# Own SBUF buffers for weight sums made by transfers, with masks and temporaries moved between SBUF regions, in a two-layer hybrid attention and SwiGLU kernel

## The chip, the cores and the metric

The kernel runs on one core of one Trainium2 chip. The metric is the device time of one execution in microseconds (us). A core has a matrix engine (TensorE, "PE" in the profile), a vector engine (VectorE, "DVE"), an activation engine (ScalarE, "ACT"), a general engine (GpSimd, "POOL") and a queue engine (SyncE, "SP"). Each works through its own instructions in the order that the program gave them. Data moves between the device memory and the on-chip memory SBUF by DMA. Plain transfers are issued on SP here; transfers that add to what lies in SBUF are issued on POOL. PE writes into PSUM, which the code divides into eight banks.

## What is computed

Two layers (`DEPTH = 2`) work on 256 tokens of width 2048, in float32. Each has a token mixer of two attention groups, an output projection, a layer norm, a SwiGLU feed-forward part (FFN) of width 5632, and a second layer norm.

```python
def reference(x, positions, w_in, ...):
    for i in range(DEPTH):
        mix = _hybrid_mixer(x, positions, w_in[i], ...)
        x = _layer_norm(ALPHA * x + mix, ln1_g[i], ln1_b[i])
        ffn = _swiglu(x, w_gate[i], w_up[i], w_down[i])
        x = _layer_norm(ALPHA * x + ffn, ln2_g[i], ln2_b[i])
    return x

def _swiglu(x, w_gate, w_up, w_down):
    h = jax.nn.silu(jnp.einsum('bsd,df->bsf', x, w_gate)) * jnp.einsum('bsd,df->bsf', x, w_up)
    return jnp.einsum('bsf,fd->bsd', h, w_down)
```

The mixer makes one input projection. Group A is attention over the 64 best keys that a small indexer picks for each query; group B is latent attention, in which the latent vectors `cq` and `ckv` are normalised by their root mean square and projected up to queries, keys and values.

## The kernel before

**Three products for one.** A float32 matmul is made of matmuls on parts: `split` (L361) and `parts` (L309) have ACT round a tile to a high part (`wh`, `xh`) and DVE subtract it to get the low part (`wl`, `xl`). Each product is then high x high, high x low and low x high, three matmuls on PE into one PSUM bank (L339 to L341 in projections, L921 to L924 in the FFN's first half).

**Weights.** A weight unit is 128 x 1024 float32 (512 KB, two blocks of 128 rows by 512 columns). `load_raw` (L303) takes a buffer under the tag `raw` and loads it on SP (L306); `parts` turns it into `wh` and `wl` (L317 on ACT, L318 on DVE), buffers of the tags `wh` and `wl`. `raw` has four buffers in the pool `sb`, which lives for the whole kernel. In the phase `more` (FFN and the end of the output projection) two more `raw` lie in that phase's own pool, and `some` (L295) decides in turn whether a unit gets one of the four or one of the two.

**Phases.** `turn(name)` (L100) closes the pool of the last phase and opens the next one in the same part of SBUF: `att` for attention, `more` for the rest of the layer. A buffer of the new phase can be written only when what lay there is done with. `pt` (L109) takes tiles in `att`. Temporaries of 2 KB in a partition come from `t2` (L116): five buffers in `sb`, and in the phase `att` six more, given out in turn. In the FFN the temporaries are the down projection's `d`, the gains `g` and `b`, and the operands `av` and `sv` of the sums on the token side.

**The FFN.** The 5632 hidden columns go in 11 chunks of 512. For chunk 0 gate and up are plain projections. For the other chunks `gate_up` works in quads. A quad takes blocks of two k units (`u` and `u + HALF`) of gate and up for both token tiles. A plain quad (`N`) makes eight products of two k blocks. A summed quad (`S`, `wino_quad`, L947) makes seven products by a Strassen-Winograd scheme, from sums of weights and sums of tokens. It needs four weight tiles: `r12`, which is the up weights of `u` plus those of `u + HALF`, and three plain ones, `r11`, `r21`, `r22`. `r12` is loaded plainly on SP, and then a second transfer on POOL adds the other unit to it (L951). DVE forms the further sums in place: L975 writes `r12 + r11` to `r11`, L979 and L987 the next two. Each of the seven tiles goes through `parts` and then into six matmuls. Chunk 1 has the order NNNS, chunk 2 NSNS, the other eight SSNS.

The last quad of a chunk also combines the products in PSUM into gate and up (`on`, L961, writing `g` and `e`), which frees the banks. `hidden` (L883) then applies SiLU, multiplies and transposes. From chunk 3 on, `down_half` puts a part of the down projection ahead of each chunk: two of four output columns, each of four units, for a pair of earlier chunks. Its results go from PSUM by ACT to `d` (L1025), and POOL issues a transfer that adds `d` to `x` (L1026).

**Attention.** `cmask` and `selmask` (128 x 256) are the causal masks; they lie in the pool `const` for the whole kernel and are made once by `constants()` (L175), called after the first projection of layer 0. Latent vectors are normalised (`rms`, L570), transposed on PE and split by `rms_out` (L584) into `ckvT` and `cqT`; `dup_out` (L555) writes `kpT` from the same PSUM bank as `ckvT`. The indexer's many small DVE operations run in the same stretch.

**Order.** A scheduler lays the instructions of each engine in a fixed order before the run. It goes by the order of the program as a priority, raised by `tc.high_priority(offset=n)`, by when inputs and buffers are free in its own model, and inserts all waits. `tasks` (L264) are generators by which pieces of attention and of norms are laid between the units of projections.

Of the kernel before, what the change touches and what calls it, by code (L numbers as in the profile page):

```python
# [23 lines left out]
F32 = mybir.dt.float32  # L24
# [7 lines left out]
P = 128  # L32
D = 2048
S = 256
# [20 lines left out]
NFC = FFN // C  # L55
RAW = 4
UNITS, MORE = 5, 3
RAWMORE = 2
HALF = NKT // KU // 2
SOONER = 60  # L60
SOON = 200
FIRSTD = 3
T2, T2MORE = 5, 6


QI0, TA, QI1, TB, KA0, QA0, VA0, KA1, QA1, VA1 = range(10)
# [14 lines left out]
def hybrid_trunk(ctx: ExitStack, tc: tile.TileContext, x, xt_in, pos, w_in, g_cq, g_ckv, w_uq,  # L81
# [8 lines left out]
    def nm(s):  # L90
        uid[0] += 1
        return f"{s}{uid[0]}"
# [73 lines left out]
            nc.sync.dma_start(xt[t], x[t * P:(t + 1) * P, :])  # L166

    ident = const.tile([P, P], F32, name="ident")
    cmask = const.tile([P, S], F32, name="cmask")
    selmask = const.tile([P, S], F32, name="selmask")  # L170
    mhalf = const.tile([P, 1], F32, name="mhalf")

    make_identity(nc, ident)

    def constants():  # L175
        nc.gpsimd.memset(cmask, 0.0)
        nc.gpsimd.affine_select(out=cmask[:, P:], in_=cmask[:, P:], compare_op=ALU.is_ge, fill=MASKED,
                                base=0, pattern=[[-1, P]], channel_multiplier=1)
        nc.vector.tensor_scalar(selmask, cmask, 1.0 / 3.0, -BIG, ALU.mult, ALU.add)
        nc.gpsimd.memset(mhalf, -0.5)  # L180

    def causal(m, t):
        return m if t else m[:, P:]
# [119 lines left out]
    def load_raw(src, n):  # L303
        pool, bufs = some("raw", RAW, RAWMORE)
        raw = pool.tile([P, KU * C], F32, name=nm("raw"), tag="raw", bufs=bufs)
        nc.sync.dma_start(raw[:, :n], src)  # L306
        return raw

    def parts(raw, n, own=None):  # L309
# [51 lines left out]
    def split(hi, lo, src):  # L361
        nc.scalar.activation(hi, src, AF.Copy)
        nc.vector.tensor_tensor(lo, src, f(hi), op=ALU.subtract)
# [148 lines left out]
    def layer(l, xh, xl, norms, last):  # L512
# [70 lines left out]

        def rms_out(n, dst, t, tp):  # L584
            tv = tp[:, :n].rearrange("p (k t) -> p k t", t=P)
            split(dst[:, 0, :, t * P:(t + 1) * P], dst[:, 1, :, t * P:(t + 1) * P], tv)

        def tb_post(o):
            gq = t2([P, QL], "gq")
# [21 lines left out]
        def indexer():  # L611
            yield from behind(p_ta, p_qi0, p_qi1)
            score = [pt([P, P * (t + 1)], F32, f"score{t}") for t in range(NT)]
            for t in range(NT):
                n = P * (t + 1)
                per = C // n
                for h0 in range(0, I_HEADS, 2 * per):
                    rp = att()
                    for j in range(per):
                        for r in range(2):  # L620
                            h = h0 + 2 * j + r
                            pr = slice(64 * r, 64 * r + 64)
                            mm(rp[:, r, j * n:(j + 1) * n], qiT[h // 8][pr, h // 2 % 4, t * P:(t + 1) * P],
                               kiT[pr, :n], start=True, stop=True)
                    rl = []
                    for r in range(2):
                        s = t2([P, per, n], "rel")
                        nc.scalar.activation(s.rearrange("p j n -> p (j n)"), rp[:, r, :], AF.Relu)
                        rl.append(s)
                    for j in range(per):  # L630
                        for r in range(2):
                            h = h0 + 2 * j + r
                            nc.vector.scalar_tensor_tensor(
                                score[t], rl[r][:, j, :], wi[t][:, h:h + 1],
                                causal(cmask, t) if h == 0 else score[t], op0=ALU.mult, op1=ALU.add)
                    yield 2
            for t in range(NT):
                for _ in range(TOPK // 8):
                    m8 = small([P, 8], "m8")
                    nc.vector.max(m8, score[t])  # L640
                    nc.vector.match_replace(score[t], m8, score[t], TAKEN)
                    yield 1
                nc.vector.tensor_scalar(bias[t], score[t], (MASKED + TAKEN) / 2, BIG, ALU.is_le, ALU.mult)
                nc.vector.tensor_tensor(bias[t], bias[t], causal(selmask, t), op=ALU.add)

        def cqk(t, k):
            return cqT[:, 0, k, t * P:(t + 1) * P], cqT[:, 1, k, t * P:(t + 1) * P]
# [34 lines left out]
        def mla_attend(hp, m, wait, *before):  # L682

            yield wait
            yield from behind(*before)
            qn, kn, vb = m
            if "B" not in oT:
                oT["B"] = [t8([P, M_HEADS, S], F32R, "oB") for _ in range(2)]

            def logits(h0, dst):  # L690


                ts = [slice(t * P, (t + 1) * P) for t in range(NT)]
                for j in range(2):
                    for t in range(NT):
                        h = (h0 + j) % 4
                        mm(dst[j][t], qn[:, h, ts[t]], kn[:, h, :P * (t + 1)], start=t == 0, stop=False)
                for t in range(NT):
                    for j in range(2):
                        pr = slice(64 * j, 64 * j + 64)  # L700
                        mm(dst[j][t], qpT[pr, h0 // 2, ts[t]], kpT[pr, :P * (t + 1)], start=False, stop=t == NT - 1)

            h0 = 2 * hp
            yield from attend(logits, M_SCALE, [causal(cmask, t) for t in range(NT)],
                              lambda h: (vb[:, 0, (h % 4) * P:(h % 4 + 1) * P], vb[:, 1, (h % 4) * P:(h % 4 + 1) * P]),
                              oT["B"][0][:, h0:h0 + 2, :], oT["B"][1][:, h0:h0 + 2, :], h0)

# [36 lines left out]
        qi_whole = t8([P, I_HEADS // 2, S], F32, "qiT")  # L744
        qiT = [qi_whole[:, 0:4, :], qi_whole[:, 4:8, :]]
        if l == 0:
            o = in_chunk(QI0, load_xT)
            constants()
            rope_tables()
        else:  # L750
            o = in_chunk(QI0, None, lambda: finish(*norms))
        p_qi0 = spawn(heads_T(o, 8, I_DIM, I_ROT, cosI, sinI, qiT[0]))
        turn("att")
        kiT, kpT = pt([P, S], F32, "kiT"), pt([P, S], F32, "kpT")
        wi = [pt([P, I_HEADS], F32, "wi", bufs=2) for _ in range(NT)]
        cq = [pt([P, QL], F32, "cq", bufs=2) for _ in range(NT)]
# [148 lines left out]
        def gate_up(fc, order, between):  # L905
# [40 lines left out]

            def wino_quad(u, final):  # L947
                ADD, SUB = ALU.add, ALU.subtract

                r12 = load_raw(w_gu[1][l, fc, u], KU * C)  # L950
                nc.gpsimd.dma_start(r12, w_gu[1][l, fc, u + HALF], accum_op=ADD)  # L951
                r11, r21, r22 = (load_raw(w_gu[i][l, fc, v], KU * C) for i, v in ((0, u), (0, u + HALF), (1, u + HALF)))

                def p(i, lhs, raw, ks):
                    w = parts(raw, KU * C)
                    name = INTO.get(i, i)
                    passes(name, lhs, ks, w, final)

                def on(d, x, y, op):
                    with tc.high_priority(offset=SOONER):  # L960
                        nc.vector.tensor_tensor(d, x, y, op=op)  # L961

                if final:
                    e = phase["pool"].tile([P, NT, C], F32, name=nm("e"), tag="e", bufs=1)
                    g = phase["pool"].tile([P, NT, C], F32, name=nm("g"), tag="silu", bufs=1)
                lo_, hi_ = unit(u), unit(u + HALF)
                p("p1", token(0), r11, lo_)
                if final:
                    with tc.high_priority(offset=SOONER):
                        nc.scalar.activation(e[:, 0, :], o["p1"], AF.Copy)  # L970
                p("p2", token(0), r21, hi_)
                if final:
                    on(g[:, 0, :], e[:, 0, :], o["c11"], ADD)
                tick()
                nc.vector.tensor_tensor(r11, r12, r11, op=ADD)  # L975
                p("p6", slhs("s2"), r11, lo_)
                if final:
                    on(e[:, 0, :], o["p6"], e[:, 0, :], SUB)
                nc.vector.tensor_tensor(r21, r11, r21, op=ADD)  # L979
                p("p7", slhs("s3"), r12, lo_)  # L980
                if final:
                    on(e[:, 1, :], e[:, 0, :], o["p7"], ADD)
                tick()
                p("p4", token(1), r21, hi_)
                if final:
                    on(g[:, 1, :], o["c21"], e[:, 1, :], SUB)
                nc.vector.tensor_tensor(r11, r11, r22, op=SUB)  # L987
                p("p5", slhs("s1"), r11, lo_)
                if final:
                    on(e, e, o["p5"].unsqueeze(1).to_broadcast([P, NT, C]), ADD)  # L990
                tick()
                p("p3", slhs("s4"), r22, lo_)
                if final:
                    on(e, e, o["up"], ADD)
                tick()
                if final:
                    return g, e
# [141 lines left out]
```

## Time and profile before

| | us |
|---|---|
| median of 3 runs (2223.49 to 2227.57) | 2225.21 |
| the profiled execution | 2224.56 |
| its span | 2222.8 |
| PE busy in it | 2169.5 |
| DVE busy | 1739.8 |
| ACT busy | 1233.2 |
| POOL busy | 154.4 |

The slices of the page show the DMA engines' mean busy share and the bytes per second in 40 equal stretches of 55.6 us:

```profile
DMA  8544456667787787778845445665687787787885
GB/s 297 168 161 152 152 188 216 201 189 229 230 239 222 227 259 220 234 224 231 252 141 162 162 155 186 199 210 199 189 243 238 236 244 239 225 259 219 252 289 140
```

How to read the views: a row of instructions has the line in the code, the engine, the operation and what it writes and reads by the program's tile names; `xN` is the count. In brackets or behind an arrow stands how long the engine was idle just before, and what released it. A row of a waits view says who waited for whom, the total in us, how often, and the longest. A row of the view by stages has the stretch, its length, each engine's busy time with its number of instructions, PE's granted clock, the busy share of the DMA engines and the GB/s.

### The profile page before, as it was taken

What the parts mean: (1) busy time and instruction counts of PE and PEld (TensorE: products, weight loads), DVE (VectorE), ACT (ScalarE), POOL (GpSimd) and SP (SyncE); (2) the same over time, 40 slices, a digit from 0 to 9 for tenths busy, and PEclk for the clock granted to TensorE, in tenths of its full rate; (3) what the DMA queues carried; (4) which work ended last, traced back from release to release, by engine and by line L of the source; (5) the groups of instructions that cost most, each with busy time, mean ns of one, the idle gap of its engine ahead of it and who ended that gap; (6) DMA issues with size and microseconds to landing.
All of it is one profiled execution on the core that took longest, in us unless ns stands there. A gap on an engine that the chain in (4) does not pass through costs nothing. (4 is left out here: it accounts for less than half of the span.)

```text
span 2222.8 us, 28085 instructions
## 1 busy us (share of the span) xinstructions
PE 2169.5 (98%) x10044; PEld 1787.7 (80%) x10044; DVE 1739.8 (78%) x2226; ACT 1233.2 (55%) x1619; POOL 154.4 (7%) x252
## 2 busy tenths in 40 slices
PE   8999999999999999999999999999999999999997
PEld 7888888888777877877888888888888778877776
DVE  6685557898887889888666857678898888889885
ACT  5555554655555566556455555446565566556653
POOL 0100000100000110100101000000001000110101
PEclk9999999999999999999999999999999999999999
DMA  8544456667787787778845445665687787787885
GB/s 297 168 161 152 152 188 216 201 189 229 230 239 222 227 259 220 234 224 231 252 141 162 162 155 186 199 210 199 189 243 238 236 244 239 225 259 219 252 289 140
DMA packets 136365, 471.15 MB, mean 212 GB/s; under 512 B 15408, under 2 KB 15712, under 8 KB 135584
## 3 DMA queue, kind: packets, MB, share of 16 engines
q1 hardware_dynamic: 113760, 409.13, 54.4%
q0 software_dynamic: 22320, 60.09, 14.1%
q8 instruction: 79, 1.29, 0.2%
q14 instruction: 62, 0.51, 0.1%
q10 hardware_dynamic: 144, 0.13, 0.0%
HBM read 445.69 MB, written 2.10 MB: 201 GB/s over the span
## 5 line engine op out<-in xcount | busy, mean ns | idle before, releaser
L317 ACT ACTIVATE wh<-raw 128x1024 fp32r<-128x1024 f32 (+1 forms) x918 | 944.0, 1053 | 809.5 <-PE acc L341 213.3
L318 DVE TENSOR_TENSOR wl<-raw,wh 128x1024 fp32r<-128x1024 f32 (+1 forms) x918 | 1093.5, 1217 | 292.7 <-ACT wh L317 289.6
L339 PE MATMUL acc<-wh,xh 128*128 128x512 f32 (+1 forms) x768 | 304.1, 396 | 6.2 <-ACT wh L317 6.2
L341 PE MATMUL acc<-wh,xl 128*128 128x512 f32 (+1 forms) x768 | 298.9, 389 | 0.5 <-DVE xl L405 0.5
L340 PE MATMUL acc<-wl,xh 128*128 128x512 f32 (+1 forms) x768 | 298.3, 388 | 0.0
L339 PE MATMUL acc<-wh,hT 128*128 128x512 f32 x640 | 252.9, 395 | 18.9 <-DVE e L961 16.6
L341 PE MATMUL acc<-wh,hT 128*128 128x512 f32 x640 | 249.9, 391 | 0.0
L340 PE MATMUL acc<-wl,hT 128*128 128x512 f32 x640 | 249.8, 390 | 0.0
L339 PEld LDWEIGHTS acc<-wh,xh 128*128 128x128 f32 x768 | 145.4, 189 | 37.0 <-ACT wh L317 6.2
L341 PEld LDWEIGHTS acc<-wh,xl 128*128 128x128 f32 x768 | 145.2, 189 | 29.2 <-DVE xl L405 1.3
L340 PEld LDWEIGHTS acc<-wl,xh 128*128 128x128 f32 x768 | 145.4, 189 | 27.2 <-DVE wl L318 1.2
L923 PE MATMUL gu_c<-wl,xh 128*128 128x512 f32 x424 | 165.4, 390 | 0.3 <-DVE wl L318 0.3
L921 PE MATMUL gu_c<-wh,xh 128*128 128x512 f32 x424 | 165.0, 389 | 0.0
L924 PE MATMUL gu_c<-wh,xl 128*128 128x512 f32 x424 | 165.0, 389 | 0.0
L339 PEld LDWEIGHTS acc<-wh,hT 128*128 128x128 f32 x640 | 120.4, 188 | 55.3 <-ACT wh L317 18.2
L341 PEld LDWEIGHTS acc<-wh,hT 128*128 128x128 f32 x640 | 120.6, 188 | 25.4
L975 DVE TENSOR_TENSOR raw<-raw,raw 128x1024 f32<-128x1024 f32 x54 | 66.1, 1223 | 94.9 <-DMA raw<-in_w_up_dram 94.9
L340 PEld LDWEIGHTS acc<-wl,hT 128*128 128x128 f32 x640 | 120.6, 188 | 24.1
L951 POOL DMA_DIRECT2D raw<-in_w_up_dram x54 | 46.1, 853 | 988.8 <-DMA raw<-in_w_up_dram 435.9
L923 PE MATMUL gu_p<-wl,many 128*128 128x512 f32 x228 | 90.8, 398 | 9.2 <-DVE wl L318 9.1
L923 PEld LDWEIGHTS gu_c<-wl,xh 128*128 128x128 f32 x424 | 79.6, 188 | 18.4 <-DVE wl L318 1.9
L921 PEld LDWEIGHTS gu_c<-wh,xh 128*128 128x128 f32 x424 | 79.6, 188 | 16.6
(285 smaller groups left out, 3424.3 us busy)
## 6 DMA issues: line engine op xcount, KB each, us to landing
raw<-in_w_gate_dram SPq DMA_DIRECT2D x176, 512.0 KB, 5.5
raw<-in_w_up_dram SPq DMA_DIRECT2D x176, 512.0 KB, 5.1
raw<-in_w_down_dram SPq DMA_DIRECT2D x176, 512.0 KB, 5.0
raw<-in_w_in_dram SPq DMA_DIRECT2D x144, 512.0 KB, 3.5
raw<-in_w_o_dram SPq DMA_DIRECT2D x64, 512.0 KB, 4.2
raw<-in_w_up_dram POOLq DMA_DIRECT2D x54, 512.0 KB, 8.1
x<-d POOLq DMA_DIRECT2D x80, 256.0 KB, 7.8
raw<-in_w_in_dram SPq DMA_DIRECT2D x16, 400.0 KB, 3.1
```

What stands on the lines that cost most here:

```text
L317: nc.scalar.activation(wh[:, :n], raw[:, :n], AF.Copy)
L318: nc.vector.tensor_tensor(wl[:, :n], raw[:, :n], f(wh[:, :n]), op=ALU.subtract)
L339: mm(o[t][:, :n], h, a, start=first, stop=False)
L340: mm(o[t][:, :n], h, b, start=False, stop=False)
L341: mm(o[t][:, :n], l, a, start=False, stop=final)
L921: mm(o[name], h, a, start=name not in begun, stop=False)
L923: mm(o[name], h, b, start=False, stop=False)
L924: mm(o[name], l, a, start=False, stop=end)
L951: nc.gpsimd.dma_start(r12, w_gu[1][l, fc, u + HALF], accum_op=ADD)
L975: nc.vector.tensor_tensor(r11, r12, r11, op=ADD)
```

## The change

Four things change.

- In `more` the plain `raw` buffers are four and one instead of four and two. The tile `r12` no longer comes from them: `load_sum` takes it from two buffers of their own, tag `sum`, in that phase's pool, with the same two transfers.
- The temporaries of `t2` are four in `sb` and seven in `att`, instead of five and six.
- The masks move from `const` to the pool of `att`, and `make_masks` builds them in each layer. For this, `turn("att")` stands ahead of the first projection in layer 0, and in layer 1 behind it but ahead of the heads' rotation.
- The splits in `rms_out` get a higher priority (`SOON` is 200).

```diff
 UNITS, MORE = 5, 3
-RAWMORE = 2
+RAWMORE, RAWSUM = 1, 2
...
-T2, T2MORE = 5, 6
+T2, T2MORE = 4, 7
...
-    cmask = const.tile([P, S], F32, name="cmask")
-    selmask = const.tile([P, S], F32, name="selmask")
+    masks = {}
...
-    def constants():
+    def make_masks():
+        cmask, selmask = (pt([P, S], F32, s) for s in ("cmask", "selmask"))
+        masks.update(c=cmask, sel=selmask)
         nc.gpsimd.memset(cmask, 0.0)
...
         nc.vector.tensor_scalar(selmask, cmask, 1.0 / 3.0, -BIG, ALU.mult, ALU.add)
-        nc.gpsimd.memset(mhalf, -0.5)
...
+    def load_sum(a, b):
+
+        raw = phase["pool"].tile([P, KU * C], F32, name=nm("sum"), tag="sum", bufs=RAWSUM)
+        nc.sync.dma_start(raw, a)
+        nc.gpsimd.dma_start(raw, b, accum_op=ALU.add)
+        return raw
...
         def rms_out(n, dst, t, tp):
             tv = tp[:, :n].rearrange("p (k t) -> p k t", t=P)
-            split(dst[:, 0, :, t * P:(t + 1) * P], dst[:, 1, :, t * P:(t + 1) * P], tv)
+            with tc.high_priority(offset=SOON):
+                split(dst[:, 0, :, t * P:(t + 1) * P], dst[:, 1, :, t * P:(t + 1) * P], tv)
...
         if l == 0:
+            turn("att")
             o = in_chunk(QI0, load_xT)
-            constants()
+            nc.gpsimd.memset(mhalf, -0.5)
+            make_masks()
             rope_tables()
         else:
             o = in_chunk(QI0, None, lambda: finish(*norms))
+            turn("att")
+            make_masks()
         p_qi0 = spawn(heads_T(o, 8, I_DIM, I_ROT, cosI, sinI, qiT[0]))
-        turn("att")
...
             def wino_quad(u, final):
                 ADD, SUB = ALU.add, ALU.subtract
-
-                r12 = load_raw(w_gu[1][l, fc, u], KU * C)
-                nc.gpsimd.dma_start(r12, w_gu[1][l, fc, u + HALF], accum_op=ADD)
+                r12 = load_sum(w_gu[1][l, fc, u], w_gu[1][l, fc, u + HALF])
```

The three uses of the masks (the indexer's first head, the selection, the latent attention) read `masks["c"]` and `masks["sel"]` instead.

More of the change, by code (lines that the diff above doesn't have):

```diff
@@ L634, in indexer @@
                                 score[t], rl[r][:, j, :], wi[t][:, h:h + 1],
-                                causal(cmask, t) if h == 0 else score[t], op0=ALU.mult, op1=ALU.add)
+                                causal(masks["c"], t) if h == 0 else score[t], op0=ALU.mult, op1=ALU.add)
                     yield 2
@@ L643, in indexer @@
                 nc.vector.tensor_scalar(bias[t], score[t], (MASKED + TAKEN) / 2, BIG, ALU.is_le, ALU.mult)
-                nc.vector.tensor_tensor(bias[t], bias[t], causal(selmask, t), op=ALU.add)
+                nc.vector.tensor_tensor(bias[t], bias[t], causal(masks["sel"], t), op=ALU.add)
         def cqk(t, k):
@@ L703, in mla_attend @@
             h0 = 2 * hp
-            yield from attend(logits, M_SCALE, [causal(cmask, t) for t in range(NT)],
+            yield from attend(logits, M_SCALE, [causal(masks["c"], t) for t in range(NT)],
                               lambda h: (vb[:, 0, (h % 4) * P:(h % 4 + 1) * P], vb[:, 1, (h % 4) * P:(h % 4 + 1) * P]),
```

## The prediction, made before the changed kernel was run

> **What bounds the kernel now.** I read the page first, its busy times and the slices.
>
> ```profile
> span 2222.8 us, 28085 instructions
> PE 2169.5 (98%) x10044; PEld 1787.7 (80%) x10044; DVE 1739.8 (78%) x2226; ACT 1233.2 (55%) x1619; POOL 154.4 (7%) x252
> raw<-in_w_up_dram SPq DMA_DIRECT2D x176, 512.0 KB, 5.1
> raw<-in_w_up_dram POOLq DMA_DIRECT2D x54, 512.0 KB, 8.1
> x<-d POOLq DMA_DIRECT2D x80, 256.0 KB, 7.8
> ```
>
> PE is busy 98% of the span, which looks as if nothing were left. But the ends of matmuls are modelled, so I count starts instead. The timeline of PE around one of the weight sums:
>
> ```profile
> 699.90 0.39 PE L921 MATMUL att<-wh,xh 128*128 128x512 f32 x1
> ...
> 707.84 0.39 PE L924 MATMUL gu_c<-wh,xl 128*128 128x512 f32 x1
> 708.36 0.50 PE L921 MATMUL gu_p<-wh,many 128*128 128x512 f32 x1
> 709.61 0.50 PE L923 MATMUL gu_p<-wl,many 128*128 128x512 f32 x1 [0.76 <-DVE wl L318]
> ```
>
> A matmul of 512 columns lasts 0.39 us in the record, but the next one starts sooner: the first two rows are 35 starts apart without a gap, 7.94 us, so **0.227 us** for each. The gap printed at 709.61 is 0.76 us; by starts PE lost 1.25 - 0.23 = 1.02 us there. So lost PE time is found by counting. The view by stages over most of the two FFNs (520:1080 is layer 0, 1640:2160 layer 1), then two single chunks of layer 0:
>
> ```profile
> 520.00:1080.00 560.00, 539.40 (x2367) 435.46 (x2367) 471.67 (x434) 321.92 (x362) 51.56 (x60) 1.00 0.80 234
> 1640.00:2160.00 520.00, 509.80 (x2251) 416.72 (x2251) 450.20 (x412) 307.91 (x341) 50.66 (x60) 1.00 0.81 243
> 586.60:652.30 65.70, 63.71 (x278) 51.15 (x278) 55.57 (x52) 37.57 (x42) 6.00 (x7) 1.00 0.81 231
> 652.30:719.00 66.70, 63.86 (x279) 51.30 (x279) 55.96 (x52) 37.20 (x42) 6.03 (x7) 1.00 0.79 227
> ```
>
> One chunk is three summed quads (7 products of 6 matmuls), one plain quad (48), two down columns (96) and 8 transposes: 270 matmuls and 8 transposes, the 278 of the third row. At 0.227 us, and 0.11 us for a transpose (the rows at 118.30 to 119.04 below: 7 in 0.74 us), that is 61.3 + 0.9 = 62.2 us, against 65.7 and 66.7 measured. The same count over the long stretches, with 8 transposes in each 278: 528.8 us of work in 560 and 503.4 in 520. **PE loses 31.2 us in the first and 16.6 us in the second, 47.8 together.** Who causes it is in the views of the waits: PE's (first two rows) and DVE's, and DVE's for the same two stretches (the last two pairs, layer 0 then layer 1):
>
> ```profile
> PE acc L339 <- DVE e L961: 16.6, 13, 1.9
> PE gu_p L923 <- DVE wl L318: 9.1, 15, 1.2
> ...
> DVE raw L975 <- DMA raw<-in_w_up_dram: 94.9, 32, 5.7
> ...
> DVE raw L975 <- DMA raw<-in_w_up_dram: 45.0, 14, 5.7
> DVE wl L318 <- ACT wh L317: 36.5, 25, 2.8
> ...
> DVE raw L975 <- DMA raw<-in_w_up_dram: 44.7, 16, 4.9
> DVE wl L318 <- ACT wh L317: 22.4, 22, 3.0
> ```
>
> In these stretches PE waits for DVE nearly always, and DVE's largest own wait is for the sum that L951's accumulating DMA makes. One case, on POOL's, DVE's and PE's timelines:
>
> ```profile
> 694.71 0.85 POOL L951 DMA_DIRECT2D raw<-in_w_up_dram  x1 [18.09 <-DVE wl L318]
> ...
> 705.90 1.22 DVE L975 TENSOR_TENSOR raw<-raw,raw 128x1024 f32<-128x1024 f32 x1 [5.70 <-DMA raw<-in_w_up_dram]
> ...
> 718.11 0.68 DVE L961 TENSOR_TENSOR e<-gu_p,e 128x512 f32<-128x512 f32 x1
> ...
> 718.94 0.47 PE L339 MATMUL acc<-wh,hT 128*128 128x512 f32 x1 [0.76 <-DVE e L961]
> ```
>
> DVE stands 5.70 us for the sum. PE then loses 1.02 us at 709.61, and after the quad the down projection waits at 718.94 for `e<-gu_p,e`, which frees its bank and which DVE, now late, runs only at 718.11. Both PE rows above are one cause: DVE has 55.6 to 56.0 us of work in a chunk of 62.2, so its 5 us of sum waiting have nowhere to go.
>
> A second, small bound lies in attention. ACT's, DVE's and PE's timelines, PE's waits, and the granted clock by stages:
>
> ```profile
> 112.83 0.37 ACT L362 ACTIVATE ckvT<-tr 128x256 fp32r<-128x256 f32 x1
> 117.97 0.28 ACT L556 ACTIVATE kpT<-tr 128x128 f32<-128x128 f32 x1 [4.29 <-DVE ckvT L363]
> 117.52 0.42 DVE L363 TENSOR_TENSOR ckvT<-tr,ckvT 128x256 fp32r<-128x256 f32 x1
> 118.30 0.44 PE L359 MATMUL tr<-ident,rn 128*128 128x128 f32 x2 [1.89 <-ACT kpT L556]
> 118.58 0.27 PE L359 MATMUL tr<-ident,dup 128*128 128x128 f32 x1
> 118.68 0.60 PE L359 MATMUL tr<-ident,rn 128*128 128x128 f32 x4
> 119.04 0.47 PE L339 MATMUL acc<-wh,xh 128*128 128x512 f32 x1
> ...
> PE tr L359 <- ACT kpT L556: 3.8, 2, 1.9
> ...
> 120.00:160.00 40.00, 40.00 (x219) 34.27 (x219) 33.09 (x79) 22.93 (x37) 0.00 (x0) 0.96 0.47 156
> 1200.00:1240.00 40.00, 38.13 (x197) 31.09 (x194) 35.84 (x98) 22.70 (x43) 4.93 (x8) 0.96 0.43 145
> 1800.00:1840.00 40.00, 38.19 (x160) 30.82 (x159) 32.89 (x31) 21.03 (x25) 1.88 (x3) 0.96 0.74 234
> ```
>
> DVE's half of the split of `ckvT` could start at 113.2, when ACT's half ended, but it sits behind indexer work until 117.52; ACT's `kpT` waits for it, and PE for ACT, once in each layer.
>
> **The change part by part.**
>
> *Own buffers for the sums.* Instructions and bytes stay the same (54 accumulating DMAs, their 54 plain loads); only when they start moves. A sum now takes its landing (8.1 us after the plain load's 5.1, together over 13 us) in a buffer that comes free when the second-last sum has been split, more than a plain quad's 48 x 0.227 = 10.9 us before it is needed and mostly a whole down phase before. The load can go out that early only if the order on SP lets it overtake plain loads. The order of before does such things:
>
> ```profile
> L176 POOL MEMSET cmask<- x1: 315/315/315, 0.9 to 0.9; 128x256 f32 x1
> L177 POOL TENSOR_SCALAR_AFFINE_SELECT cmask<-cmask x1: 284/284/284, 1.5 to 1.5; 128x128 f32<-128x128 f32 x1
> L179 DVE TENSOR_SCALAR selmask<-cmask x1: 286/286/286, 11.9 to 11.9; 128x256 f32<-128x256 f32 x1
> ```
>
> The code writes this memset after the whole first projection, and it ran at 0.9 us: what has its buffer and its inputs goes. So I expect the 94.9 us of DVE waiting to nearly vanish. What is late next is DVE itself. In layer 0 its idle time is 560 - 471.67 = 88.3 us, 43.3 without the sums, or 5.1 in each of 2367/278 = 8.5 chunks; 55.5 of work and 5.1 of idle make 60.6 us against PE's 62.2. In layer 1 it is (69.8 - 44.7)/8.1 = 3.1 and 55.6, so 58.7. PE becomes the bound, by a margin of 1.6 to 3.5 us per chunk: thin, so I take not all of the 47.8 but two thirds, **-31.9 us**. The ends are 0 (no load moves) and -47.8.
>
> *Five plain buffers for six.* A sum held one of the six for over 13 us, so a quad loses nothing. In the down phase a buffer is taken for 5.3 us (median to landing), ACT's 1.06 and DVE's 1.22, 7.6 us; five of them give a unit each 1.5 us, and PE needs one in 12 x 0.227 = 2.7. Even at the slowest landing it is 13.0/5 = 2.6. I take 0; if that cover goes, it is a few tenths in a chunk.
>
> ```profile
> DMA to landing us min/median/max: 3.0/5.3/10.7
> L317 ACT ACTIVATE wh<-raw x253: 1037/1055/1079, 559.0 to 1057.9; 128x1024 fp32r<-128x1024 f32 x127
> ```
>
> *Priority for the splits of the latent vectors.* DVE's `ckvT` moves from 117.52 to about 113.2. PE keeps the 1.89 us, twice 3.8 by its waits. The clock falls to 0.96 in both stages, (1 - 0.96) x 40 = 1.6 us each, right behind the stall; if the stall makes it, that is 3.2 more. Ends 0 and -7.0; the clock seems to follow the stall, as the third such stage (1800:1840) also holds a DVE wait of PE, but only some stalls of this size have a fall behind them. I take **-5.5**. The Trainium skill, "TensorE: Matmul & The Clock Gate", section "HAM oscillation — how this bites in real kernels", speaks against that: it asks for no idle gap over some 3.4 us, and 1.89 is well below; by it the falls are not the stall's, this part brings at most the 3.8, and the sum would be 1.7 us longer. The trace has a fall behind both stalls.
>
> *Masks in attention's part, built in each layer.* One more memset, select and scaling, 0.32 + 0.28 + 0.29 us. In layer 1 POOL's two wait until the FFN's buffers are free; behind them stand only the gains' loads, whose users come tens of us later, and PE needs none of it before the indexer. I take 0; uncovered it would be +0.9.
>
> *Temporaries.* In attention 4 + 7 is 11 as 5 + 6 was. The first projection of layer 0 gets 11 where it had 5, so its x loads go out a little earlier among the weight loads: 0, at most 1 either way. In the FFN there are four for five; `d` is the user. A `d` lives 7.8 us in its DMA, two are made per column of 10.9 us, so two to four are enough. 0, and the rival below if not.
>
> The profiled run took 2224.56 us, 0.65 below the median of 2225.21, and the sum starts from it: 2224.56 - 31.9 - 5.5 = **2187.2 us**.
>
> **Rivals.**
>
> *The plain loads become the wait.* The chunk moves the same bytes with DMA at 0.80, and early sums now run beside plain loads that are needed sooner. For it: ACT and through it DVE already wait for plain loads (36.5 us and 22.4 us above). Against it: the sums run beside plain loads now too, and leave more even traffic. If it halves the gain: 2224.56 - 16 - 5.5 = 2203. The Trainium skill, "DMA: Bandwidth & Descriptors", section "Queues, rings and completion order", lets each DMA engine take turns between queues, so an early sum would take its turn from an urgent plain load; it bears on this rival.
>
> *The sum loads do not move.* If SP's order keeps them where they are, only the splits gain: 2224.56 - 5.5 = 2219. Against it stand the mask rows above.
>
> *Slower: POOL's queue and the fourth temporary.* POOL works in order. An accumulate put early at its head waits for its plain load, and `x<-d` stands behind it; ACT then finds no free `d` and all conversions behind it wait. Four `d` cover two columns, 21.8 us, so this decides from a hold of 21.8 - 7.8 = 14 us on; five covered 2.5 columns. POOL's idle times before L951 reach such lengths (18.09 us above), though there with nothing ready behind. At 3 us in each of 18 chunks: 2187 + 54 = 2241, and the result is slower than before from 2.1 us per chunk on.
>
> **How the numbers follow.** Forecast 0.70 (2187, by itself 2174 to 2198: nine tenths of the 47.8 and all of the 7.0 at one end, under half at the other), halved gain 0.12 (2203), unmoved 0.09 (2219, half of it within 0.2%), slower 0.09 (2241). 0.2%, 4.4 us, is about what a measurement of this kernel can tell from no change. Faster 0.70 + 0.12 + 0.04 = 0.86, same 0.05, slower 0.09. The range leaves out the slower case and most of the unmoved one: 2173 to 2215.
>
> **What would show it.** DVE's wait at L975 falls from 94.9 to under 15 us; the accumulating DMAs are issued 10 us or more ahead of L975; PE's rows for `e` and `wl` fall from 25.7 to under 8; chunks take 62 to 64 us; `kpT` and the 0.96 of 120:160 and 1200:1240 are gone. I am wrong if sums are early and chunks still take over 65 us (then DVE's wait for `wh` has grown), if PE shows waits for `d`, or if L975 waits as before.

## The result, and the profile after

The changed kernel takes 2186.88 us (median of 4 runs, 2184.32 to 2196.58) against 2224.35 us before (median of 4): a ratio of **0.9839, 95% interval 0.9812 to 0.9867**. The profiled run is the slowest of the four, 2196.58 us, 28.0 below the profiled run of before. Code lines have moved: the projections' three matmuls are L346 to L348 (were L339 to L341), the conversions L324 and L325 (L317, L318), the sum's accumulating transfer L313 (L951), the first use of the sum L984 (L975), `e` and `g` L970 (L961), `kpT` L563 (L556), `d` L1034 (L1025).

The view of L984, the operation that DVE stood before for 94.9 us, with what its engine waited for under "its engine sat idle before it":

```profile
L984 DVE TENSOR_TENSOR raw<-sum,raw x54: 1216/1222/1227, 458.3 to 2103.2; 128x1024 f32<-128x1024 f32 x54
...
its engine sat idle before it (us, times) until:
who waited for it (us, times):
  ACT wh L324: 103.7, 37
```

Nothing stands under the heading: in 54 uses DVE never waited for a sum. One sum of layer 0, on SP's, POOL's and DVE's timelines:

```profile
679.40 0.33 SPq L312 DMA_DIRECT2D sum<-in_w_up_dram  x1
...
684.24 0.85 POOL L313 DMA_DIRECT2D sum<-in_w_up_dram  x1 [9.86 <-DVE wl L325]
...
725.18 1.22 DVE L984 TENSOR_TENSOR raw<-sum,raw 128x1024 f32<-128x1024 f32 x1
```

The plain load goes out 45.8 us before the sum is used, ahead of plain loads that are used sooner, and the accumulate 40.9 us before, where it was 11.2 us (694.71 to 705.90) in the case of before. Over all 54 sums the accumulate's lead, from its issue to the first use, is 18.6 us or more with a median of 35.6; before it was at most 13.3 us, with a median of 9.5.

The stages of the two FFNs (each window 20 us shorter than before's, to stay inside the FFN), and PE's and DVE's waits:

```profile
520.00:1060.00 540.00, 535.08 (x2389) 441.70 (x2388) 472.66 (x433) 325.14 (x360) 49.71 (x58) 1.00 0.81 242
1620.00:2120.00 500.00, 490.85 (x2179) 403.89 (x2178) 435.65 (x400) 298.01 (x330) 47.10 (x56) 1.00 0.81 241
...
PE acc L346 <- DVE e L970: 13.5, 9, 4.3
...
PE tr L366 <- ACT kpT L563: 3.5, 2, 1.9
PE att L932 <- DVE e L970: 1.3, 1, 1.3
PE gu_p L932 <- ACT d L1034: 0.7, 1, 0.7
PE att L934 <- DVE wl L325: 0.4, 1, 0.4
...
DVE wl L325 <- ACT wh L324: 347.8, 252, 6.0
```

At 62.2 us for 278 matmuls and transposes, 2389 and 2179 of them are 534.5 and 487.5 us of work: PE loses 5.5 and 12.5 us. By the same 62.2 us it lost 30.4 in 560 and 16.4 in 520 before, which is 29.3 and 15.8 in windows of this length. So some 27 us came back, nearly the whole 28.0 us between the two profiled runs; the first sum is used at 458.3 us in both, so the attention ahead of it gave nothing. It came back almost only in layer 0 (23.8 us). In layer 1 DVE's 44.7 us of waiting for sums went as well, but only 3.3 us of PE's loss.

The `wl` row shrank from 9.1 to 0.4 us, but the `e` row only from 16.6 to 13.5. What DVE now waits for is ACT's `wh` (347.8 us, 289.6 before). ACT's waits for the FFN's plain loads, the first block before, the second after:

```profile
ACT wh L317 <- DMA raw<-in_w_gate_dram: 125.5, 84, 4.4
ACT wh L317 <- DMA raw<-in_w_up_dram: 61.4, 20, 6.0
...
ACT wh L317 <- DMA raw<-in_w_down_dram: 29.9, 37, 2.9
```

```profile
ACT wh L324 <- DMA raw<-in_w_down_dram: 80.8, 57, 6.2
ACT wh L324 <- DMA raw<-in_w_up_dram: 72.8, 36, 6.1
ACT wh L324 <- DMA raw<-in_w_gate_dram: 71.0, 60, 4.1
```

Together they hardly moved, 216.8 us before and 224.6 after. What changed is where they fall: from the gate loads to those of the down projection, which land later now. The median times to landing, the first row before, the second after:

```profile
raw<-in_w_down_dram SPq DMA_DIRECT2D x176, 512.0 KB, 5.0
```

```profile
raw<-in_w_down_dram SPq DMA_DIRECT2D x176, 512.0 KB, 6.1
```

By the issues and landings in the two traces, 104 of the 176 down loads are now under way together with an accumulate of a sum, 36 before. These 104 landed after 7.6 us in the median, the other 72 after 4.8.

How such a wait reaches PE, in the worst case of this run, on SP's, POOL's, ACT's, DVE's and PE's timelines:

```profile
1661.62 12.20 SPq L306 DMA_DIRECT2D raw<-in_w_down_dram  x6
...
1663.12 0.85 POOL L313 DMA_DIRECT2D sum<-in_w_up_dram  x1 [19.60 <-DVE wl L325]
...
1671.16 1.06 ACT L324 ACTIVATE wh<-raw 128x1024 fp32r<-128x1024 f32 x1 [6.20 <-DMA raw<-in_w_down_dram]
...
1666.81 0.69 DVE L970 TENSOR_TENSOR e<-gu_p,e 128x512 f32<-128x512 f32 x1
1672.24 1.22 DVE L325 TENSOR_TENSOR wl<-raw,wh 128x1024 fp32r<-128x1024 f32 x1 [4.75 <-ACT wh L324]
1673.39 0.68 DVE L970 TENSOR_TENSOR e<-e,gu_p 128x512 f32<-128x512 f32 x1
...
1674.12 0.65 PE L346 MATMUL acc<-wh,hT 128*128 128x512 f32 x1 [4.30 <-DVE e L970]
```

The load that ACT waits for is the second of the six: it went out at 1662.92, when a plain buffer came free, and landed at 1671.05, 8.13 us later. The accumulate of a sum that is not needed yet went out 0.20 us after it and landed at 1671.25. By the trace's DMA packets of 4 KB, SP's queue starts 29 of them from 1667 to 1669 and POOL's 77; from 1671 to 1673, with the accumulate done, SP's queue starts 203. So the load lands late, ACT and DVE wait, and DVE has the last `e` operation, which frees the bank of `p7`, behind that one conversion. PE stands 4.30 us.

### The profile page after: what moved, and what is told of

Same layout as the page of the kernel before. It is cut to its first block, busy times and chain, and to the rows that moved or that the text cites. A ratio compares the mean times of both kernels' runs of the same rounds, so it can differ in the third digit from the quotient of the medians.

```text
span 2194.5 us, 28019 instructions
## 1 busy us (share of the span) xinstructions
PE 2157.3 (98%) x10044; PEld 1790.1 (82%) x10044; DVE 1741.2 (79%) x2227; ACT 1238.0 (56%) x1619; POOL 156.0 (7%) x254
## 4 chain that ended last, share of the span: by engine, by line
PE 66%; DVE 12%; issue 9%; DMA 9%; ACT 2%; POOL 1%; POOLq 0%; ACTq 0%; DVEq 0%; SPq 0%
PE acc L346 14%; PE acc L348 14%; PE acc L347 14%; DVE wl L325 7%; DMA raw<-in_w_gate_dram 4%; DMA raw<-in_w_down_dram 3%; PE tr L366 2%; ACT wh L324 2%; PE gu_p L932 2%; PE gu_p L935 2%; PE gu_p L934 2%; PE gu_c L932 2%; PE gu_c L935 2%; PE gu_c L934 2%; PE att L932 1%
## 5 line engine op out<-in xcount | busy, mean ns | idle before, releaser
L324 ACT ACTIVATE wh<-raw 128x1024 fp32r<-128x1024 f32 (+1 forms) x864 | 896.4, 1054 | 750.8 <-PE acc L348 208.1
L325 DVE TENSOR_TENSOR wl<-raw,wh 128x1024 fp32r<-128x1024 f32 (+1 forms) x864 | 1035.0, 1218 | 352.4 <-ACT wh L324 347.8
L346 PE MATMUL acc<-wh,xh 128*128 128x512 f32 (+1 forms) x768 | 304.1, 396 | 6.0 <-ACT wh L324 6.0
L348 PE MATMUL acc<-wh,xl 128*128 128x512 f32 (+1 forms) x768 | 298.6, 389 | 0.0
L346 PE MATMUL acc<-wh,hT 128*128 128x512 f32 x640 | 251.4, 393 | 13.7 <-DVE e L970 13.5
L348 PE MATMUL acc<-wh,hT 128*128 128x512 f32 x640 | 249.8, 390 | 0.0
L346 PEld LDWEIGHTS acc<-wh,xh 128*128 128x128 f32 x768 | 145.2, 189 | 36.5 <-ACT wh L324 6.0
L348 PEld LDWEIGHTS acc<-wh,xl 128*128 128x128 f32 x768 | 144.9, 189 | 28.9 <-DVE xl L412 0.8
L346 PEld LDWEIGHTS acc<-wh,hT 128*128 128x128 f32 x640 | 120.5, 188 | 44.0 <-DVE e L970 18.5
L348 PEld LDWEIGHTS acc<-wh,hT 128*128 128x128 f32 x640 | 120.6, 188 | 25.3
L313 POOL DMA_DIRECT2D sum<-in_w_up_dram x54 | 46.2, 856 | 906.5 <-DVE wl L325 396.3
L1035 POOL DMA_DIRECT2D x<-d x80 | 74.3, 1070 | 495.5 <-ACT d L1034 490.9
L935 PEld LDWEIGHTS gu_c<-wh,xl 128*128 128x128 f32 x424 | 79.6, 188 | 16.7
L934 PEld LDWEIGHTS gu_c<-wl,xh 128*128 128x128 f32 x424 | 79.6, 188 | 16.6
```

Of the source, the lines that this page charges most:

```text
L313: nc.gpsimd.dma_start(raw, b, accum_op=ALU.add)
L324: nc.scalar.activation(wh[:, :n], raw[:, :n], AF.Copy)
L325: nc.vector.tensor_tensor(wl[:, :n], raw[:, :n], f(wh[:, :n]), op=ALU.subtract)
L346: mm(o[t][:, :n], h, a, start=first, stop=False)
L348: mm(o[t][:, :n], l, a, start=False, stop=final)
L934: mm(o[name], h, b, start=False, stop=False)
```

## The experiments

The theory after the result, **A**: a sum in a buffer of its own starts early, DVE no longer stands for it, and PE gets the time. Its rivals: **B**, the seventh buffer brings it, whoever uses it; **C**, the masks, temporaries and the priority bring it. Two more came up on the way: **D**, what is left of PE's loss are banks that are freed late; **E**, it is plain loads that come late.

**e1, the sums' buffers in the same room.** Before, with `load_sum`, four plain buffers and two for the sums.

```diff
-RAWMORE = 2
+RAWMORE, RAWSUM = 0, 2
...
-                r12 = load_raw(w_gu[1][l, fc, u], KU * C)
-                nc.gpsimd.dma_start(r12, w_gu[1][l, fc, u + HALF], accum_op=ADD)
+                r12 = load_sum(w_gu[1][l, fc, u], w_gu[1][l, fc, u + HALF])
```

> Before, with only the sums' two own buffers: four plain ones and two for the sums, six in all as before; masks, temporaries and priorities as before. Theory A (a sum of its own buffer starts early, and DVE no longer stands for it): DVE's 94.9 us of waiting at the first sum fall under 15 us, and the time comes to 2187 to 2202, a little above the changed kernel since only four plain buffers are left. Theory B (the seventh buffer is what counts): 2220 to 2235. Theory C (masks, temporaries and priority bring it): 2224 or slower.

Measured: 2267.49 us, 1.0191 of before (1.0150 to 1.0232). DVE's wait at the first sum (here L981) was nil, as A says, and yet the kernel was 42 us slower. PE's, DVE's and ACT's waits:

```profile
PE acc L346 <- DVE e L967: 59.0, 22, 4.3
...
DVE wl L325 <- ACT wh L324: 419.0, 286, 5.4
...
ACT wh L324 <- DMA raw<-in_w_down_dram: 132.5, 104, 4.9
```

With four plain buffers ACT waits for the down projection's loads 104 times, and PE's largest row is `e`. That is not the whole loss: the mean granted clock is 0.981 in this run's profile and 0.996 in before's, and (1 - 0.981) x 2276.7 - (1 - 0.996) x 2222.8 = 34 us, so up to 34 of the 54 us between the two profiled runs are the slower clock. Of its 17 falls, 16 begin within 2 us of the end of one of PE's stalls on `e`. A's mechanism held; its price for the missing plain buffer did not. By its time alone the run would also fit C's "or slower", so C is left to e4.

**e2, seven shared buffers.** The changed kernel, but sums take plain buffers again, of which there are four and three.

```diff
-RAWMORE, RAWSUM = 1, 2
+RAWMORE = 3
...
-                r12 = load_sum(w_gu[1][l, fc, u], w_gu[1][l, fc, u + HALF])
+                r12 = load_raw(w_gu[1][l, fc, u], KU * C)
+                nc.gpsimd.dma_start(r12, w_gu[1][l, fc, u + HALF], accum_op=ADD)
```

> The changed kernel, but the sums take their buffer from the plain ones again, of which there are seven: the same room in SBUF as in the changed kernel. Theory A: the sum's load still queues in turn among the plain loads, one buffer ahead of before; DVE's wait at the first sum falls only in part, to 40 to 70 us, and the time is 2205 to 2218. Theory B: under 15 us of waiting and 2187. Theory C: 2187 with the waits of before.

Measured: 2225.34 us, 1.0011 (0.9998 to 1.0024). DVE's wait at the first sum:

```profile
  DMA raw<-in_w_up_dram: 111.8, 25
```

It did not even fall. B is out: the same room without ownership brings nothing. A was too kind to it as well; that a seventh shared buffer lets the sum start no earlier than its turn would explain it, but is not shown.

**e3, one buffer for the sums, six plain.**

```diff
-RAWMORE, RAWSUM = 1, 2
+RAWMORE, RAWSUM = 2, 1
```

> The changed kernel with six plain buffers and one for the sums (seven in all). Theory A: the second of two sums in a row cannot start before the first is split; its two transfers need over 13 us and DVE wants it some 8 us later, so DVE waits about 5 us once in a chunk, 70 to 100 us in all, and the time is 2205 to 2220. Theory B: 2187 or a little less.

Measured: 2235.89 us, 1.0042 (1.0029 to 1.0054), slower than before. DVE's wait at the first sum, and PE's first row:

```profile
  DMA sum<-in_w_up_dram: 86.2, 20
```

```profile
PE gu_p L934 <- DVE wl L325: 17.4, 22, 1.8
```

20 waits of 4.3 us, about one in a chunk, as A worked out from the second of two sums in a row. The time is 16 us worse than A's range. PE's `wl` row is nearly twice before's 9.1, which is half of that; the rest was not traced.

**e4, all but the sums' own buffers.** Masks, temporaries and priority as changed; four and two plain buffers, shared with the sums.

```diff
-RAWMORE, RAWSUM = 1, 2
+RAWMORE = 2
...
-                r12 = load_sum(w_gu[1][l, fc, u], w_gu[1][l, fc, u + HALF])
+                r12 = load_raw(w_gu[1][l, fc, u], KU * C)
+                nc.gpsimd.dma_start(r12, w_gu[1][l, fc, u + HALF], accum_op=ADD)
```

> The changed kernel without the sums' own buffers: four and two plain ones, shared with the sums as before; masks, temporaries and the splits' priority as changed. Theory A: DVE's wait at the first sum stays at 85 to 105 us and the time is 2219 to 2226. Theory C: 2187 to 2200.

Measured: 2228.76 us, 1.0010 (0.9993 to 1.0026), with 92.1 us of waiting at the first sum. C is out: the side changes by themselves are worth nothing. What they do is make room: two masks of 1 KB and one temporary of 2 KB in each partition leave the FFN's part of SBUF, and that is the 4 KB of the seventh weight buffer. e1 shows what the sums' own two are worth without it.

**e5, the changed kernel again**, beside the next three on another chip.

> The changed kernel once more, beside the next three on one chip. 2184 to 2197; DVE has no wait at the first sum, PE's rows for e come to 9 to 18 us, kpT's to 3.5.

Measured: 2195.83 us (2193.73 to 2195.99), 0.9883 (0.9855 to 0.9911). The interval overlaps the first one; runs of this kernel lie up to 12 us apart.

**e6, without the splits' priority.**

```diff
-            with tc.high_priority(offset=SOON):
+            if True:
                 split(dst[:, 0, :, t * P:(t + 1) * P], dst[:, 1, :, t * P:(t + 1) * P], tv)
```

> The changed kernel without the higher priority of the splits in rms_out. The prediction gave the priority 5.5 us, so by it 2192; by the changed kernel's trace, where DVE's ckvT still starts at 117.13 and kpT waits 4.28 us as before, the priority does nothing and the time is that of the changed kernel within 2 us, with PE waiting 3.5 to 3.8 us for kpT.

Measured: 2196.76 us, 0.9872 (0.9828 to 0.9917): the same as e5. The place in the changed kernel, on DVE's, ACT's and PE's timelines:

```profile
117.13 0.42 DVE L370 TENSOR_TENSOR ckvT<-tr,ckvT 128x256 fp32r<-128x256 f32 x1
...
117.58 0.28 ACT L563 ACTIVATE kpT<-tr 128x128 f32<-128x128 f32 x1 [4.28 <-DVE ckvT L370]
...
117.91 0.69 PE L366 MATMUL tr<-ident,rn 128*128 128x128 f32 x2 [1.88 <-ACT kpT L563]
```

The `ckvT` of this row, the first token tile's, has the same place in DVE's order before, with the priority and without it: 4 us of other operations stand between ACT's half of the split and it. Only the second token tile's `ckvT` moves up, by one operation of 0.48 us. So on the chip DVE reaches that place late. Why the scheduler left it there is not shown; a model in which DVE gets there earlier, so that a priority has nothing to move, would explain it.

**e7, e8, e9: other banks.** In e7 the down projection's first column takes the banks of `p1` and `p6`, its second those of `p7` and `p5`; e8 also lays the second token tile's transposes one unit later (`yield 1 + t` in `tb_post`); e9 is e8 with hidden's transposes in the banks of `c11` and `c21`, from the chunk ahead of the first down projection on.

```diff
-                          ... (0, 1) if i % 2 else (2, 3))
+                          ... (3, 0) if i % 2 else (1, 2))
...
-        BANKS = {"c11": 4, "c21": 5, "p1": 0, "p5": 1, "p6": 2, "p7": 3}
+        BANKS = {"c11": 4, "c21": 5, "p1": 1, "p5": 0, "p6": 2, "p7": 3}
...
-        turns["acc"] = 1
+        turns["acc"] = 0
...
-                yield 1
+                yield 1 + t
...
-                tp = bank(2 + t, "tr")
+                tp = bank(b0 + t, "tr")
...
-            held.append((fc, hT, spawn(hidden(g, u, hT, wait))))
+            held.append((fc, hT, spawn(hidden(g, u, hT, wait, 2 if fc + 1 < FIRSTD else 4))))
```

> The changed kernel, where the down projection's first column takes the banks of p1 and p6 in place of p6 and p7, and its second those of p7 and p5. Theory D (what PE still loses in a chunk is the wait for p7's bank, which DVE reads behind a conversion whose weights landed late): PE's rows for e fall from 13 to under 4 us and the time by 6 to 14 us, to 2173 to 2181. If DVE itself is the bound, the wait moves to PE's next use of DVE's tiles and the time stays at 2187.

> As e7_banks, and the second token tile's transposes of the latent vectors come one unit (12 matmuls, 2.7 us) later. If PE's 3.5 us for kpT come from DVE being 4 us behind at that place, they vanish and the time is 3 to 7 us below e7_banks; if the chain itself is too long, PE waits at the later place and the time is that of e7_banks.

> As e8_banks_later_t1, but hidden's transposes take the banks of c11 and c21, which were read a whole down column before. Theory D (PE's remaining loss is banks freed late, by DVE for p7 and, in e7 and e8, by ACT's d): no row of PE for e, and under 4 us for d; the time is 10 to 16 us below that of e5, 0.980 to 0.985 of before. If DVE or ACT themselves are the bound, the lost 20 us move on to PE's waits for wh, wl or hT and the time stays at 0.988.

Measured: e7 2201.04 us, 0.9909 (0.9878 to 0.9940); e8 2195.11 us, 0.9881 (0.9848 to 0.9914); e9 2186.30 us, 0.9817 (0.9791 to 0.9843). In all three the `e` row is gone, and another has come. PE's waits in e7, and in e9:

```profile
PE tr L366 <- ACT d L1034: 21.6, 10, 7.6
...
PE tr L366 <- ACT kpT L563: 3.5, 2, 1.9
```

```profile
PE gu_c L932 <- DVE hT L370: 10.2, 8, 2.4
```

In e7 hidden's transposes meet a bank that ACT's `d` frees late. In e9 the banks are free, and PE waits for DVE's `hT`. e9's figures are those that D foresaw (no row for `e` or `d`, 0.980 to 0.985), but e10 below reaches the same time without the bank moves, and that is why D falls. PE finds DVE or ACT late at the next place where it meets them; that both are late because they wait for weights is what e11 tries. In e8 the `kpT` row is gone, and e8 is 5.9 us below e7 on the same chip, though the intervals touch.

**e10, the later transposes alone**, on the changed kernel, and **e11, seven plain buffers** and two for the sums, paid for with one of the eight pairs `wh`, `wl`.

```diff
-UNITS, MORE = 5, 3
-RAWMORE, RAWSUM = 1, 2
+UNITS, MORE = 5, 2
+RAWMORE, RAWSUM = 3, 2
```

> The changed kernel with the second token tile's transposes one unit later, and nothing else: PE's 3.5 us for kpT vanish with the clock's fall that may follow them (1.7 us each); 4 to 7 us below e5, 0.985 to 0.987 of before.

> The changed kernel with seven plain buffers in place of five, paid for with one of the eight pairs wh, wl. Theory E (after the sums, the plain loads are what DVE waits for, through ACT): ACT's waits for raw, 225 us by the changed kernel's trace, fall under 160, and the time by 3 to 10 us. If the lead that eight pairs give is needed more, the time rises by 5 us or more.

Measured, on one chip with e9: e10 2186.06 us, 0.9824 (0.9800 to 0.9848); e11 **2173.93 us, 0.9765 (0.9738 to 0.9793)**. e10 takes the same time as e9, so the bank moves are worth nothing that could be measured; its `kpT` row is gone. Its 0.9824 lies below the 0.985 to 0.987 that were expected, and is clear only of e5's interval, which is from another chip; with the first measurement's 0.9839 it overlaps. e11's stages, PE's waits and ACT's largest for plain weights of the FFN:

```profile
520.00:1060.00 540.00, 540.00 (x2420) 447.88 (x2419) 474.23 (x434) 327.80 (x363) 51.19 (x60) 1.00 0.82 243
1620.00:2120.00 500.00, 499.32 (x2234) 413.49 (x2234) 443.32 (x408) 304.06 (x338) 45.99 (x56) 1.00 0.83 249
...
PE acc L346 <- ACT wh L324: 6.7, 2, 6.0
PE tr L366 <- ACT kpT L563: 3.5, 2, 1.9
...
ACT wh L324 <- DMA raw<-in_w_gate_dram: 50.7, 21, 6.6
...
ACT wh L324 <- DMA raw<-in_w_down_dram: 16.0, 10, 3.1
```

2420 at 62.2 us per 278 are 541.4 us of work in 540, and 2234 are 499.8 in 500: PE loses nothing in the FFN any more, and no row for `e` is left. E holds: ACT's waiting for the FFN's plain loads fell from 224.6 us to the 66.7 of these two rows, the down loads' share from 80.8 to 16.0, and the eighth pair was not needed. 119 of the 176 down loads are still under way together with an accumulate, so the sums' transfers did not make way; that with seven buffers the loads go out early enough fits this. The time fell by 12 us against e10, more than the 3 to 10 that were expected.

**e12, e11 and e10 together.**

> e11 and e10 together: seven plain buffers, two for the sums, seven pairs wh, wl, and the second token tile's transposes one unit later. In e11 PE lost nothing to e any more and kept 3.5 us for kpT; these go: 2 to 5 us below e11, 0.974 to 0.976 of before.

Measured: **2170.64 us, 0.9747 (0.9726 to 0.9769)**, faster than before and than the changed kernel. PE's waits, all of them:

```profile
PE acc L346 <- ACT wh L324: 6.1, 2, 5.9
PE acc L348 <- DVE xl L412: 0.5, 1, 0.5
PE acc L346 <- DVE xh L411: 0.3, 1, 0.3
PE tr L366 <- DVE lg L485: 0.2, 1, 0.2
```

## Why the prediction was right, and where its terms were not

The time came to 2186.88 us against 2187.0, but that the figures meet is partly luck: three terms were off (the sums' gain, the plain buffers, the priority) and make up for each other.

- **Own buffers for the sums, -31.9 us.** The mechanism is shown. The wait went from 94.9 to 0 (forecast under 15), and the loads overtake the others, by 40.9 us in the case above, so that the rival in which they do not move is out. The size is not: no run shows this part by itself, but with seven plain buffers beside it PE's whole loss in the FFN goes (e11, 52.6 us below before on that chip). The third that was taken off for caution stands, as far as these runs tell, for what the missing plain buffers took back. With four plain buffers this part makes the kernel slower (e1), which no part of the prediction allowed for. A slip in the sum is small: at 62.2 us the stretch of layer 0 holds 529.6 us of work and not 528.8, and PE's loss before is 46.8 us and not 47.8.
- **Five plain buffers for six, 0 us.** This step failed. It took a buffer to be held for landing and two conversions, 7.6 us, and found 1.5 us a unit against PE's 2.7. In the changed kernel's trace a down load holds its buffer for 10.8 us in the median, from its issue to the end of DVE's part (168 loads whose conversion the semaphore records name), and 35 of the 168 for more than 13.5 us, which is what five buffers at 2.7 us cover. Landing takes longer beside the sums' accumulates, 7.6 us, and a landed tile also waits for its turn on ACT and DVE, of which DVE has work for 88% of the time (472.66 of 540 us). The runs show four plain buffers at 1.0191, much of it clock, five at 0.9839 and 0.9883, seven at 0.9765. Five instead of seven cost 12 us between e10 and e11, and 15 us between e10 and e12, which differ only in the buffers and one pair `wh`, `wl`. So the rival of late plain loads was at work inside the forecast. The argument against it, that the sums ran beside plain loads before too and would now leave more even traffic, came out the other way: 36 down loads met an accumulate before and 104 after. It is also why PE's `e` and `wl` rows came to 15.2 us (13.5, 1.3 and 0.4) where under 8 were forecast.
- **Priority for the splits, -5.5 us.** Wrong: nothing (e6 against e5, and the `kpT` row of 3.5 us after 3.8). The stall was read rightly, its remedy was not; the later transposes of e8, e10 and e12 remove it. Of the clock's share, layer 1 kept a stall of 1.61 us, 1.87 before, and lost its fall, and layer 0 kept both. On the clock gate the Trainium skill's limit of some 3.4 us of idling ("TensorE: Matmul & The Clock Gate", section "HAM oscillation — how this bites in real kernels") does not decide it by itself: the 1.88 us in layer 0 had a fall behind it (0.97 and 0.98 in 80:120 and 120:160), the 1.61 us in layer 1 had none (1.00). Nor does the length alone: in the profiles of before, the changed kernel, e1 to e7 and e11 this stall lasted 1.87 to 1.89 us twelve times, with a fall behind it in five, and 1.59 to 1.61 us eight times, with none. The rows of the changed kernel:

```profile
80.00:120.00 40.00, 38.12 (x221) 32.12 (x220) 32.97 (x85) 23.85 (x45) 4.93 (x8) 0.97 0.53 172
120.00:160.00 40.00, 40.00 (x223) 34.49 (x222) 33.19 (x79) 22.53 (x36) 0.00 (x0) 0.98 0.47 156
1160.00:1200.00 40.00, 40.00 (x232) 34.70 (x231) 32.19 (x85) 24.82 (x44) 6.99 (x10) 1.00 0.54 173
1200.00:1240.00 40.00, 38.39 (x224) 32.74 (x223) 35.39 (x87) 22.95 (x39) 0.00 (x0) 1.00 0.52 172
```

- **Masks and temporaries, 0 us.** Right (e4), and the slower rival by way of `d` did not come: PE's only row for `d` is 0.7 us.
- **Chunks of 62 to 64 us.** 540/(2389/278) = 62.8 and 500/(2179/278) = 63.8 us: right, against 65.8 and 64.2 by the same count before.

What stays open: why runs of the changed kernel lie up to 12 us apart. e6's profiled run of 2180.31 us has 4.4 us for `e` where the changed kernel's of 2196.58 has 13.5, so late plain loads may be part of it; but e5's run of 2195.82 has only 9.4, and what makes loads late in one run and not in the next was not tried.

## What to carry to other kernels

A tile that needs two transfers in a row should not wait its turn in a ring of buffers for single transfers: two buffers of its own let it start long ahead, and its wait goes. But what starts early then moves beside loads that are needed sooner. The ring that is left must be counted again, with the landing time under that traffic and the time that a landed tile waits for its engines; four, five and seven buffers were 2% slower, 1.2 to 1.6% faster and 2.4% faster here. And here moving the place where an engine meets a late partner only renamed the wait (e7 to e9), so look for what makes the partner late.

## What the hardware showed unexpectedly

After the stall of 4.30 us at 1674 the clock fell to half: by PE's timeline, the two rows below are six starts apart and 2.56 us, 0.427 us a matmul where 0.227 is usual, so these six alone cost 1.2 us on top of the stall. By 1677.87 the starts are 0.23 us apart again. In e5 a stall of 1.92 us at the same place has the same fall behind it. In e1, with 17 falls, short stalls are paid for a second time in this way in most chunks.

```profile
1674.57 0.63 PE L347 MATMUL acc<-wl,hT 128*128 128x512 f32 x1
...
1677.13 0.63 PE L347 MATMUL acc<-wl,hT 128*128 128x512 f32 x1
```
